# Two-layer S5 / RG-LRU / ConvFFN backbone: S5 parameters on stacked complex pairs, the last LRU tile beside the S5 gate, three modulation slots

## The chip, the cores and the metric

The kernel runs on one core of a Trainium2 chip. The metric is the device time of one execution in microseconds. "Before" and "after" name the two kernels. Engines: PE or TensorE (products), DVE or VectorE, ACT or ScalarE, POOL or GpSimd, SP or SyncE (which issues most of the DMAs).

## The reference

Two layers over 512 latent tokens with 256 context tokens ahead of them, width 1024. What matters here is the token mixing, which the reference computes so (cut):

```python
proj = h @ lw["w_in"]                       # u (512), x (512), g (512)
# S5: complex diagonal states, both directions
lam_bar = jnp.exp(lam * dt);  b_bar = ((lam_bar - 1.0) / lam)[..., None] * b_mat
s5_states = linear_scan(lam_bar, einsum(u, b_bar), s0, reverse)
# RG-LRU on x, both directions
xc = dwconv_seq(x_lru, conv_w, conv_b, LRU_PAD)
r, i = sigmoid(xc @ w_a + b_a), sigmoid(xc @ w_x + b_x)
log_a = (-LRU_C * r) * softplus(-lam);  a = jnp.exp(log_a)
lru_states = linear_scan(a, jnp.sqrt(-jnp.expm1(2.0 * log_a)) * (i * xc), h0, reverse)
y = gelu(s5_readout(s5_states, c_mat) + d * u)
y_s5 = y * sigmoid(y @ w_glu + b_glu)
y_lru = (lru_states[0] + lru_states[1]) * gelu(g_lru)
out = concatenate([y_s5, y_lru]) @ w_out
```

Then a post-norm, a gated feed-forward block with a 3x3 depthwise convolution, and another post-norm. Shifts, scales and gates of the norms come from `silu(c) @ w_mod + b_mod` (six vectors per layer and stream).

## The kernel before, in words

Products run as three fp32r products each (`mm3`, L165): a value is split into a high part, cast by ScalarE (L160), and a low part, the difference, by VectorE or GpSimd (L163). So L170, L171 and L172 are the three products of nearly all matrix work.

The kernel goes through its stages in order: features and modulation, token mixing of layer 0, output projection (`w_out`) and norm, the feed-forward block, and the same for layer 1. All on-chip buffers are slots of an arena (names such as `q0`, `t0`, `w6`, `e`); a slot's next user waits for its last.

S5 works in eight blocks of heads, `hb` 0 to 7. `enter` brings a block's inputs in, `prep(hb)` builds its small matrices (tables L595 to L600, a matrix that goes through DRAM as `td`), and `leave(hb)` (L714) does the complex scan: multiply by the rotations `cs` (L722 to L725, reloaded from DRAM `csd` through the one slot `t0`), two scans (L727), rotate back (L731, L732), write the states (L735 to L738), then 12 small products `yp` (L741 to L743), which ScalarE copies (L744). Every second block `store_y` sends the result to DRAM (`yd`, L648), from where the glu reloads it transposed (L962).

The RG-LRU works in four tiles l0 to l3 of 128 channels: gates by 16 products (L783) and sigmoids (L784), tanh and exp (L794, L795), root (L803), and on VectorE L798, L804, L807, scans (L809 to L812) and the sum of directions (L813); `gate` multiplies with the gelu of the projection g (L936). The projections are steps too: u0 to u3 for S5, x0 to x3 (with a convolution, L761), g0 to g3. `s` is `glu` (from L951): reload, gelu (L966), splits, then four times 24 products, two sigmoids (L977) and a multiplication (L978).

What is written where is set by the table `FILL`: one string per layer, with eight parts between bars; part hb is emitted behind `leave(hb)`. A scheduler then orders each engine's instructions by priorities: S5's blocks have 300 (`PRIO`), the fill steps none, so that the steps take the gaps of S5. Each engine, and each DMA queue, runs its list strictly in order. Between the steps a `filler` computes the modulation vectors: 16 loads of 512 KB of `w_mod` per pair of vectors through a ring of slots (m0, m1), each for four products (L185, L188).

`s5_params` (L442 to L578) makes the powers, tables and rotations of a layer: in layer 0 right at the start (`run(params, ...)`), in layer 1 chunk by chunk beside layer 0's feed-forward block. It works with real and imaginary parts as separate tiles of 128x32 and up, `cmul` (L261 to L266) being six operations; the rotations of each `hb` are six operations of 128x384 (L575 to L577).

Of the kernel before, what the change touches and what calls it, by code (L numbers as in the profile page):

```python
# [14 lines left out]
F32 = mybir.dt.float32  # L15
# [33 lines left out]
FILL = ('u1 x0 u2 u3|l0 x1||g0 l1 x2 g1|l2 x3|l3|g2|g3 s', 'x0 u1 u2 u3|l0 x1|g0 l1|x2 g1|l2 x3||l3|g3 g2 s')  # L49
# [3 lines left out]
def body(ctx: ExitStack, tc: tile.TileContext, a, out):  # L53
# [33 lines left out]
    def phase(side, *arenas):  # L87

        sides[side].close()
        pool = sides[side].enter_context(tc.tile_pool(name=side, bufs=1, side=side, reuse_waits="tile"))  # L90
        for dt, sizes in arenas:
            for n, kb in sizes.items():
                arena(pool, dt, **{n: kb})

    def mixing_phase():
        phase("left", (F32, several("a", 4, 4)), (F32, {"b": 8}))
        phase("right", (F32, several("q", 6, 3)), (F32, several("c", 2, 3)), (F32, {"w6": 4, "w7": 4}))
# [43 lines left out]
    def small(shape):  # L141
        count[0] += 1
        n = int(np.prod(shape[1:]))
        return cp.tile(list(shape), F32, name=f"{where[0]}_st_{count[0]}", tag=f"st{n}", bufs={12: 4, 4: 8, 1: 6}[n])
# [293 lines left out]
    prm = {"r8": const("r8", [128, 32]), "tab": const("tab", [128, 4, 32, 8]), "bb": const("bb", [128, 2, 33, 16]),  # L438
# [3 lines left out]
    def s5_params(l, scratch, raw_slots, phase_slots, cs_slots, tmp_slot, load=load):  # L442
# [14 lines left out]
        t = lambda: al(sh)  # L457
        (lre, lim, ldt), wre, wim = (lraw[:, i] for i in range(3)), t(), t()
        dt, are, th, mag, c1, s1, c8, s8 = (t() for _ in range(8))
        rr = dt  # L460
        t1, t2 = al([128, 32, 6]), al([128, 32, 6])
# [15 lines left out]
        reduce_angle(al, rr, th, sh)
        cos_sin(al, c8, s8, rr, sh)
# [28 lines left out]
        nr, den, q = t(), t(), t()  # L507
        V.tensor_scalar(nr, pw[:, 0, :, 1], -1.0, None, op0=ADD)
        ni = pw[:, 1, :, 1]
        V.tensor_mul(den, lre, lre)  # L510
        V.tensor_mul(q, lim, lim)
        V.tensor_add(den, den, q)
        V.reciprocal(den, den)
        V.tensor_mul(wre, nr, lre)
        V.tensor_mul(q, ni, lim)
        V.tensor_add(wre, wre, q)
        V.tensor_mul(wre, wre, den)
        V.tensor_mul(wim, ni, lre)
        V.tensor_mul(q, nr, lim)
        V.tensor_sub(wim, wim, q)  # L520
        V.tensor_mul(wim, wim, den)
        al.p = base
# [20 lines left out]
        V.tensor_copy(lo[:, 0, :, 1], c8)  # L543
        V.tensor_copy(lo[:, 1, :, 1], s8)
        v1, v2 = t1[:, :, 0], t2[:, :, 0]

        def square(o, x):
            cmul(o[0], o[1], x[0], x[1], x[0], x[1], v1, v2)
            return o

        x, y = (c8, s8), (wre, wim)
        square(y, x)
        grow(lo, 2, 0, 2, *y)
        square(x, y)
        grow(lo, 4, 0, 4, *x)
        square(y, x)
        V.tensor_copy(hi[:, 0, :, 1], y[0])
        V.tensor_copy(hi[:, 1, :, 1], y[1])
        square(x, y)
        grow(hi, 2, 0, 2, *x)  # L560
# [743 lines left out]
```

## Time and profile before

| | before |
|---|---|
| median of 3 runs | 1739.45 us (1738.14 to 1739.81) |
| profiled execution | 1738.61 us, span 1736.8 us |
| TensorE / VectorE / ScalarE / GpSimd busy | 1551.8 / 1287.7 / 672.1 / 522.7 us |
| mean granted TensorE clock | 0.938 of full |

The busy times are lengths of instructions within the span; matrix products overlap, so a busy TensorE is not one at its peak. The profiled execution is 0.84 us below the median. In the timeline a row is an instruction or a few equal ones on one engine: its start in us from the start of the span, its length, engine and line, then what it writes and reads. In square brackets stands how long the engine was idle ahead of it and what released it.

### The profile page before, as it was taken

How to read it: one execution, taken by the hardware profiler on the slowest of the kernel's cores; microseconds unless marked ns; L12 is line 12 of the kernel's file. 1: busy time of each engine (PE TensorE's matmuls, PEld its weight loads, DVE VectorE, ACT ScalarE, POOL GpSimd, SP SyncE). 2: the span in 40 equal slices, each digit the busy share in tenths (PEclk: the TensorE clock that was granted, in tenths of full speed). 3: DMA queues.
4: the chain of work that ended last, by engine and by line, in shares of the span. 5: the costliest groups of instructions: out<-in, count | busy, mean ns of one | idle time of the engine just before them, and what ended most of it. 6: DMA issues, size and time to landing. Idle time of an engine off the chain costs nothing. (4 is left out here: it accounts for less than half of the span.)

```text
span 1736.8 us, 22939 instructions
## 1 busy us (share of the span) xinstructions
PE 1551.8 (89%) x8824; PEld 1263.5 (73%) x8824; DVE 1287.7 (74%) x2244; ACT 672.1 (39%) x972; POOL 522.7 (30%) x328
## 2 busy tenths in 40 slices
PE   4997888498999999999999789989778999999996
PEld 1775666376988788887888668867456988888884
DVE  7998999368566997877689984888467575556587
ACT  3445566423633222222222236556651643323320
POOL 1000001318332222322326271000146444434374
PEclk8897888699899999999999998999879999999998
DMA  8365453522221212433334316765562233222231
GB/s 338 128 222 179 140 177 97 185 85 101 70 75 60 97 58 88 157 111 133 106 131 145 110 59 199 259 198 162 180 213 95 94 121 105 89 98 97 85 122 61
DMA packets 95358, 227.09 MB, mean 131 GB/s; under 512 B 28912, under 2 KB 39696, under 8 KB 95248
## 3 DMA queue, kind: packets, MB, share of 16 engines
q1 hardware_dynamic: 85456, 212.92, 36.6%
q10 hardware_dynamic: 9792, 12.71, 2.1%
q8 instruction: 69, 1.13, 0.3%
q14 instruction: 41, 0.34, 0.1%
HBM read 194.50 MB, written 31.10 MB: 130 GB/s over the span
## 5 line engine op out<-in xcount | busy, mean ns | idle before, releaser
L170 PE MATMUL banks<-ar,ar 128*128 128x512 f32 (+2 forms) x2152 | 774.9, 365 | 49.4 <-ACT ar L160 32.1
L171 PE MATMUL banks<-ar,ar 128*128 128x512 f32 (+2 forms) x2152 | 774.9, 361 | 16.8 <-DVE ar L396 13.1
L172 PE MATMUL banks<-ar,ar 128*128 128x512 f32 (+2 forms) x2152 | 767.8, 360 | 1.3 <-DVE ar L163 1.3
L163 POOL TENSOR_TENSOR ar<-ar,ar 128x1024 fp32r<-128x1024 f32 x148 | 364.9, 2473 | 672.8 <-ACT ar L160 596.1
L170 PEld LDWEIGHTS banks<-ar,ar 128*128 128x128 f32 x2152 | 411.1, 193 | 127.9 <-ACT ar L160 35.6
L171 PEld LDWEIGHTS banks<-ar,ar 128*128 128x128 f32 x2152 | 413.9, 192 | 80.8 <-DVE ar L396 15.1
L172 PEld LDWEIGHTS banks<-ar,ar 128*128 128x128 f32 x2152 | 413.8, 193 | 63.6 <-DVE ar L163 2.5
L160 ACT ACTIVATE ar<-ar 128x1024 fp32r<-128x1024 f32 (+2 forms) x248 | 238.9, 981 | 488.4 <-PE banks L171 212.3
L1143 DVE SCALAR_TENSOR_TENSOR ar<-banks,cols,ar 128x441 f32<-128x441 f32 (+2 forms) x352 | 243.6, 692 | 41.7 <-ACT ar L1138 35.1
L1177 DVE TENSOR_TENSOR ar<-banks,ar 128x512 f32<-128x512 f32 x160 | 109.4, 687 | 106.5 <-PE banks L172 104.5
L163 DVE TENSOR_TENSOR ar<-ar,ar 128x512 fp32r<-128x512 f32 (+2 forms) x100 | 113.6, 1148 | 81.0 <-ACT ar L160 64.3
L185 PE MATMUL banks<-ar,cond 128*32 128x256 f32 x192 | 65.9, 450 | 42.2 <-DMA ar<-in_w_mod_dram 42.2
L1150 ACT ACTIVATE ar<-ar,cols 128x768 f32<-128x768 f32 (+1 forms) x44 | 36.6, 831 | 130.5 <-DVE ar L1143 93.7
L826 POOL TENSOR_TENSOR ar<-ar 128x512 f32<-128x512 f32 x40 | 63.2, 1585 | 68.4 <-DVE ar L822 67.7
L185 PEld LDWEIGHTS banks<-ar,cond 128*32 128x32 f32 x192 | 16.2, 117 | 78.7 <-DMA ar<-in_w_mod_dram 59.6
L704 POOL MEMSET ar<- 128x8 f32 x16 | 1.9, 121 | 217.8 <-DVE ar L727 105.0
L188 PE MATMUL banks<-ar,cond 128*32 128x256 f32 x576 | 66.9, 450 | 0.0
L783 PE MATMUL banks<-ar,ar 128*128 128x512 f32 (+1 forms) x128 | 55.5, 563 | 10.3 <-ACT ar L925 5.7
L384 PE MATMUL banks<-ident,ar 128*128 128x128 f32 x176 | 36.0, 348 | 30.9 <-ACT ar L358 15.5
L396 DVE TENSOR_TENSOR ar<-ar,ar 128x256 fp32r<-128x256 f32 (+1 forms) x64 | 32.8, 531 | 31.8 <-ACT ar L395 31.7
L1138 ACT ACTIVATE ar<-banks,cols 128x512 f32<-128x512 f32 x44 | 29.9, 680 | 66.9 <-PE banks L172 66.8
L822 DVE TENSOR_TENSOR ar<-banks,ar 128x512 f32<-128x512 f32 x60 | 40.5, 681 | 18.7 <-PE banks L172 18.7
(243 smaller groups left out, 1723.3 us busy)
## 6 DMA issues: line engine op xcount, KB each, us to landing
ar<-in_w_mod_dram SPq DMA_DIRECT2D x96, 512.0 KB
ar<-in_ffn_w_up_dram SPq DMA_DIRECT2D x88, 512.0 KB
ar<-in_ffn_w_down_dram SPq DMA_DIRECT2D x44, 512.0 KB
ar<-in_w_in_dram SPq DMA_DIRECT2D x24, 512.0 KB
tabd<-ar SPq DMA_DIRECT2D x16, 512.0 KB
ar<-tabd SPq DMA_DIRECT2D x16, 512.0 KB
csd<-ar SPq DMA_DIRECT2D x16, 384.0 KB
ar<-csd SPq DMA_DIRECT2D x16, 384.0 KB
```

Source lines behind the costliest of these rows:

```text
L160: S.activation(hi, src, AF.Copy)
L163: return lo_eng.tensor_tensor(lo, src, hi.bitcast(F32), op=SUB)
L170: PE.matmul(ps, wh, xh, start=first and k == 0, stop=False)
L171: PE.matmul(ps, wh, xl, start=False, stop=False)
L172: PE.matmul(ps, wl, xh, start=False, stop=last and k == nk - 1)
L185: ins = PE.matmul(*args, **kw)
L188: ins = PE.matmul(*args, **kw)
L783: PE.matmul(gp, w[:, d, i, :], xc[:, o:o + n], start=True, stop=True)
L822: V.tensor_tensor(tmp, ps, g[:, cs], op=MUL)
L826: G.tensor_tensor(xs_t[:, cs], xs_t[:, cs], tmp, op=ADD)
L1143: inst[0] = V.scalar_tensor_tensor(av[:, yo, xo], uv[:, yi, xi], tap(1 + dy, 1 + dx, ch), av[:, yo, xo], op0=MUL, op1=ADD)
L1177: V.tensor_tensor(acc, ps, acc, op=ADD)
```

## The change

1. `s5_params` works on pairs: real and imaginary parts stand in one tile, and exp, angle, cosine and sine run on the pair of powers 1 and 8 at once. A complex product (`times`) is two multiplications over both parts and two sums; a square is three operations. Copies into the table are four for eight. For layer 0 (`sets=2`) a rotation step makes two blocks: 24 operations of 768 columns where 48 of 384 stood; `cs` lies in slot `e`, in two halves, and goes out in two stores.
2. `FILL`: in layer 0, l3 (part 5) and g2 (part 6) move into part 7, where g3 and the glu are. In layer 1, l3 moves from part 6 to 7 and g2 from 7 to 5.
3. In part 7 the products of the projections are tied behind the last product of `leave(7)`; `lru` is a generator: l3's gates are emitted at once, the rest (`lru_rest`) inside `glu`, behind the last gelu.
4. The modulation ring gets a third slot, `w7`; the gates of the LRU lose it (seven for eight).
5. `columns` takes its scratch from slot `f0`; q3, q4 and q5 become one tile; one small buffer fewer; `prep(0)` of layer 0 has a priority.

```diff
-FILL = ('u1 x0 u2 u3|l0 x1||g0 l1 x2 g1|l2 x3|l3|g2|g3 s', 'x0 u1 u2 u3|l0 x1|g0 l1|x2 g1|l2 x3||l3|g3 g2 s')
+FILL = ('u1 x0 u2 u3|l0 x1||g0 l1 x2 g1|l2 x3|||l3 g2 g3 s', 'x0 u1 u2 u3|l0 x1|g0 l1|x2 g1|l2 x3|g2||l3 g3 s')
...
+        def times(o, x, mre, mim, u1, u2):
+            V.tensor_tensor(u1, x, mre, op=MUL)
+            V.tensor_tensor(u2, x[:, ::-1], mim, op=MUL)
+            V.tensor_tensor(o[:, 0], u1[:, 0], u2[:, 0], op=SUB)
+            V.tensor_tensor(o[:, 1], u1[:, 1], u2[:, 1], op=ADD)
...
-            cmul(o[0], o[1], x[0], x[1], x[0], x[1], v1, v2)
+            v = t1[:, :, :, 0]
+            V.tensor_tensor(v, x, x, op=MUL)
+            V.scalar_tensor_tensor(o[:, 1], x[:, 0], 2.0, x[:, 1], op0=MUL, op1=MUL)
+            V.tensor_sub(o[:, 0], v[:, 0], v[:, 1])
...
-            cs = new(cs_slots[hb % 2], [128, 2, 4, 96])
-            tt = new(tmp_slot, [128, 2, 4, 96])
+            if sets > 1:
+                cs = new(cs_slots, [128, 2, 2, ng, 96])[:, h // sets % 2]
+            else:
+                cs = new(cs_slots[h % 2], [128, 2, ng, 96])
+            tt = new(tmp_slot, [128, 2, ng, 96])
...
-            nc.sync.dma_start(csd[l, hb], cs.rearrange("p i g n -> p (i g n)"))
+            for j in range(sets):
+                nc.sync.dma_start(csd[l, h + j].rearrange("p (i x) -> p i x", i=2),
+                                  cs[:, :, 4 * j:4 * j + 4].rearrange("p i g n -> p i (g n)"))
...
-            self.gates = ring(*(f"q{i}" for i in range(6)), "w6", "w7")
+            self.gates = ring(*(f"q{i}" for i in range(6)), "w6")
...
-    params = s5_params(0, "t", ("a2", "t0"), ("w6", "w7"), ("q3", "q4"), "q5", S.dma_start)
+    params = s5_params(0, "t", ("a2", "t0"), ("w6", "w7"), "e", "q3", 2, S.dma_start)
...
-        md_r = ring("m0", "m1")
+        md_r = ring("m0", "m1", "w7")
-        filler = itertools.chain(*(mods(l, q, md_r, md_r, md_b, after=first_w) for q in (1, 2)))
+        filler = itertools.chain(*(mods(l, q, md_r, md_r, md_b, 3, after=first_w) for q in (1, 2)))
+        tie = [None]
...
+            with behind(tie[0]):
+                return products(lat, ctxt, w, tag, do_ctx, parts)
...
             with tc.high_priority(PRIO2[l]):
-                hs[m] = lru(m, xcs[m], gate_b)
+                it = lru(m, xcs[m], gate_b)
+                next(it)
+            if tie[0] is None:
+                lru_rest(it, m)
+            else:
+                rest.append((it, m))
...
-                S.activation(yt, yt, AF.Gelu_apprx_tanh, bias=zero)
+                gelu = S.activation(yt, yt, AF.Gelu_apprx_tanh, bias=zero)
+            for it, m in rest:
+                with behind(gelu):
+                    lru_rest(it, m)
...
-                s5.leave(hb, fo2, tm)
+                left = s5.leave(hb, fo2, tm)
...
+                tie[0] = left if hb == 7 else None
```

Three places show how this moves the instructions. The lines of the changed kernel are its own: L726 to L742 are L722 to L738 of before, L804 to L819 are L798 to L813, L1004 and L1005 are L977 and L978.

First, VectorE at the start of layer 0's `leave(7)`, before:

```order
L809 SCALAR_TENSOR_TENSOR ar_88<-ar_82,ar_83 128x256
L812 SCALAR_TENSOR_TENSOR ar_89<-ar_84,ar_85 128x768
L810 SCALAR_TENSOR_TENSOR ar_88<-ar_82,ar_88,ar_83 128x512
L722 TENSOR_TENSOR ar_68<-ar_68 128x768
L723 TENSOR_TENSOR ar_68<-ar_68 128x768
L813 TENSOR_TENSOR ar_88<-ar_88,ar_89 128x768
L163 TENSOR_TENSOR ar_67<-ar_68,ar_67 128x1024
L724 TENSOR_TENSOR ar_68<-ar_68 128x384
L725 TENSOR_TENSOR ar_68<-ar_68 128x384
L936 TENSOR_TENSOR ar_68<-ar_68,ar_80 128x768
L727 SCALAR_TENSOR_TENSOR ar_68<-ar_68 128x384 x2
L731 TENSOR_TENSOR ar_68<-ar_68 128x768
```

and in the changed kernel:

```order
L741 TENSOR_TENSOR ar_68<-ar_68 64x4x32
L742 TENSOR_TENSOR ar_68<-ar_68 64x4x64
L726 TENSOR_TENSOR ar_68<-ar_68 128x768
L727 TENSOR_TENSOR ar_68<-ar_68 128x768
L688 TENSOR_TENSOR ar_68<-banks,dd_112 128x16
L728 TENSOR_TENSOR ar_68<-ar_68 128x384
L729 TENSOR_TENSOR ar_68<-ar_68 128x384
L731 SCALAR_TENSOR_TENSOR ar_68<-ar_68 128x384 x2
L735 TENSOR_TENSOR ar_68<-ar_68 128x768
L736 TENSOR_TENSOR ar_68<-ar_68 128x768
```

Ahead of `leave(7)` (768-wide L722, now L726) the scans of l3 no longer stand, and inside it neither L813, L163 nor the gate's product L936; `prep`'s L688 has moved into it.

Second, the glu of layer 0. VectorE in the changed kernel, between the first and second multiplications by the sigmoid (L1005):

```order
L1005 TENSOR_TENSOR ar_68<-ar_68 128x768
L810 SCALAR_TENSOR_TENSOR ar_81<-ar_83,ar_81 128x768
L810 SCALAR_TENSOR_TENSOR ar_82<-ar_86,ar_82 128x768
L813 TENSOR_TENSOR ar_83<-ar_83,ar_81 128x768
L813 TENSOR_TENSOR ar_80<-ar_80,ar_82 128x768
L815 SCALAR_TENSOR_TENSOR ar_81<-ar_83 128x256
L818 SCALAR_TENSOR_TENSOR ar_82<-ar_86,ar_80 128x768
L816 SCALAR_TENSOR_TENSOR ar_81<-ar_83,ar_81 128x512
L819 TENSOR_TENSOR ar_81<-ar_81,ar_82 128x768
L1005 TENSOR_TENSOR ar_68<-ar_68 128x768
L948 TENSOR_TENSOR ar_68<-ar_68,ar_81 128x768
```

and ScalarE at the same place (L801 is l3's exp, L809 its root, L1004 the glu's sigmoid, L163 casts):

```order
L801 ACT_TABLE_LOAD
L801 ACTIVATE ar_83<-ar_83,lru_st_2274,coef_41_524 128x768
L801 ACTIVATE ar_86<-ar_86,lru_st_2274,coef_41_524 128x768
L1004 ACT_TABLE_LOAD
L1004 ACTIVATE ar_68<-banks,cols_40_491 128x384 x2
L807 ACTIVATE lru_st_2282<-ar_86 128x1
L809 ACT_TABLE_LOAD
L809 ACTIVATE ar_81<-ar_81,lru_st_2282 128x768
L809 ACTIVATE ar_82<-ar_82,lru_st_2282 128x768
L163 ACTIVATE ar_66<-ar_68 128x1024
L163 ACTIVATE ar_67<-ar_68 128x1024
```

l3's rest now stands between the glu's multiplications; on ScalarE the glu's first two sigmoids stand between l3's exp and its root, each with a table load (ACT_TABLE_LOAD).

Third, SyncE's queue in the tail of layer 0 (`yd` is the S5 output, `gd` the modulation vectors), before:

```order
L834 DMA ar_68<-gd_107 128x1024
L200 DMA ar_68<-in_w_out_s_dram 128x1024
L962 DMA ar_68<-yd 128x8x96
L834 DMA ar_68<-gd_107 128x1024
L1037 DMA ar_68<-in_x_dram 128x1024
L200 DMA ar_68<-in_w_out_lru_dram 128x1024 x2
L962 DMA ar_68<-yd 128x8x96
L200 DMA ar_68<-in_w_out_lru_dram 128x1024 x2
```

and in the changed kernel:

```order
L694 DMA ar_76<-td 128x1x128 x4
L840 DMA ar_68<-gd_105 128x1024
L985 DMA ar_68<-yd 128x8x96
L840 DMA ar_68<-gd_105 128x1024
L985 DMA ar_68<-yd 128x8x96
L203 DMA ar_68<-in_w_out_s_dram 128x1024
L1066 DMA ar_68<-in_x_dram 128x1024 x2
L203 DMA ar_68<-in_w_out_s_dram 128x1024 x2
```

The last reload of the S5 output stood behind two loads of `in_w_out_lru` and stands ahead of them now.

## Rows read from the trace of the kernel before

**Rows 1.** The page: its span, and busy time by engine.
```profile
span 1736.8 us, 22939 instructions
...
PE 1551.8 (89%) x8824; PEld 1263.5 (73%) x8824; DVE 1287.7 (74%) x2244; ACT 672.1 (39%) x972; POOL 522.7 (30%) x328
```

**Rows 2.** Windows: length, busy us (count) of PE, weights, DVE, ACT, POOL; clock; DMA; GB/s.
```profile
286.50:295.50 9.00, 8.90 (x53) 7.70 (x52) 9.00 (x11) 6.30 (x9) 0.00 (x0) 1.00 0.18 45
300.00:350.00 50.00, 21.41 (x98) 19.50 (x99) 20.93 (x18) 18.51 (x25) 19.63 (x8) 0.64 0.49 161
340.00:358.00 18.00, 17.69 (x96) 16.37 (x95) 7.49 (x9) 9.76 (x15) 0.02 (x1) 1.00 0.16 56
550.00:600.00 50.00, 45.91 (x244) 38.60 (x243) 47.00 (x137) 14.97 (x19) 12.13 (x5) 1.00 0.20 65
...
1250.00:1300.00 50.00, 32.01 (x210) 23.23 (x203) 28.20 (x29) 32.66 (x44) 22.74 (x9) 0.76 0.62 214
```

**Rows 3.** Timeline, VectorE: start, us, engine, line, work [idle before <- what ended it].
```profile
262.83 0.95 DVE L722 TENSOR_TENSOR ar<-ar 128x768 f32<-128x768 f32 x1
...
284.36 1.83 DVE L804 SCALAR_TENSOR_TENSOR ar<-ar,ar 128x768 f32<-128x768 f32 x2 [3.81 <-ACT ar L803]
...
291.35 0.94 DVE L722 TENSOR_TENSOR ar<-ar 128x768 f32<-128x768 f32 x1
...
299.59 3.10 DVE L732 TENSOR_TENSOR ar<-ar 128x768 f32<-128x768 f32 x1
302.61 3.96 DVE L163 TENSOR_TENSOR ar<-ar,ar 128x768 fp32r<-128x768 f32 x2
...
308.48 0.42 DVE L738 TENSOR_TENSOR ar<-ar 64x256 f32<-64x256 f32 x1
```

**Rows 4.** Timeline, TensorE, the two long gaps of layer 0's tail.
```profile
307.82 0.72 PE L742 MATMUL banks<-ar,ar 128*128 128x96 f32 x2 [11.88 <-DVE ar L738]
...
331.58 1.01 PE L170 MATMUL banks<-ar,ar 128*128 128x384 f32 x2 [18.06 <-ACT ar L160]
```

**Rows 5.** Timeline, ScalarE, layer 0's tail.
```profile
282.10 1.28 ACT L803 ACT_TABLE_LOAD   x1
283.40 1.76 ACT L803 ACTIVATE ar<-ar,lru_st 128x768 f32<-128x768 f32 x2
...
313.56 0.49 ACT L744 ACTIVATE ar<-banks 128x384 f32<-128x384 f32 x1 [0.98 <-PE banks L743]
...
327.39 3.41 ACT L966 ACTIVATE ar<-ar,glu_st 128x768 f32<-128x768 f32 x4
...
340.26 1.05 ACT L977 ACTIVATE ar<-banks,cols 128x384 f32<-128x384 f32 x2 [3.33 <-PE banks L172]
```

**Rows 6.** Timeline, SyncE's queue, layer 0's tail.
```profile
322.69 0.39 SPq L962 DMA_DIRECT2D ar<-yd  x1
```

**Rows 7.** Timeline, GpSimd, beside layer 0's last `leave`.
```profile
298.93 5.95 POOL L163 TENSOR_TENSOR ar<-ar,ar 128x1024 fp32r<-128x1024 f32 x2 [24.51 <-ACT ar L160]
```

**Rows 8.** Timeline, VectorE, the end of layer 0's glu.
```profile
360.70 2.67 DVE L163 TENSOR_TENSOR ar<-ar,ar 128x512 fp32r<-128x512 f32 x2 [1.22 <-ACT ar L160]
```

**Rows 9.** Timeline, VectorE, layer 1: two `leave`s at their closest.
```profile
1089.17 0.96 DVE L722 TENSOR_TENSOR ar<-ar 128x768 f32<-128x768 f32 x1
...
1096.90 1.23 DVE L163 TENSOR_TENSOR ar<-ar,ar 128x1024 fp32r<-128x1024 f32 x1
...
1100.26 0.96 DVE L722 TENSOR_TENSOR ar<-ar 128x768 f32<-128x768 f32 x1
```

**Rows 10.** Timeline, TensorE, waits for modulation weights in layer 1's tail.
```profile
1226.49 0.63 PE L185 MATMUL banks<-ar,cond 128*32 128x256 f32 x1 [3.60 <-DMA ar<-in_w_mod_dram]
...
1254.36 0.63 PE L185 MATMUL banks<-ar,cond 128*32 128x256 f32 x1 [3.57 <-DMA ar<-in_w_mod_dram]
...
1258.65 0.64 PE L185 MATMUL banks<-ar,cond 128*32 128x256 f32 x1 [3.21 <-DMA ar<-in_w_mod_dram]
```

**Rows 11.** Groups by line and form, VectorE, 20 to 110 us, rotations.
```profile
L576 DVE TENSOR_TENSOR ar<-ar,ar 128x384 f32<-128x384 f32 x7 | 3.6, 552 | 0.0
```

More of the change, by code (lines that the diff above doesn't have):

```diff
@@ L90, in phase @@
         pool = sides[side].enter_context(tc.tile_pool(name=side, bufs=1, side=side, reuse_waits="tile"))
-        for dt, sizes in arenas:
+        for dt, sizes, *one in arenas:
+            if one:
+                arena(pool, dt, **sizes)
+                continue
             for n, kb in sizes.items():
@@ L143, in small @@
         n = int(np.prod(shape[1:]))
[L144 removed]
+        return cp.tile(list(shape), F32, name=f"{where[0]}_st_{count[0]}", tag=f"st{n}", bufs={12: 3, 4: 8, 1: 6}[n])
     load = nc.sync.dma_start
@@ L456, in s5_params @@
         al = Stack(new(scratch, [128, 2048]))
[L457 to L461, printed above, removed]
+        pair = [128, 2, 32]
+        dt, den = al(sh), al(sh)
+        pa = al([128, 2, 2, 32])
+        ang, pole, w, ws = (al(pair) for _ in range(4))
+        c18 = al([128, 2, 2, 32])
+        t1, t2 = (new(tmp_slot, [128, 2, 2, 32, 6])[:, i] for i in range(2))
         base = al.p
@@ L517, in s5_params @@
[L517 to L522, printed above, removed]
+        ri = pw[:, :, :, 1]
+        V.tensor_scalar(ri[:, 0], ri[:, 0], -1.0, None, op0=ADD)
+        V.tensor_tensor(w, lraw[:, 0:2], lraw[:, 0:2], op=MUL)
+        V.tensor_add(den, w[:, 0], w[:, 1])
+        V.reciprocal(den, den)
+        lam = [lraw[:, i].unsqueeze(1).to_broadcast(pair) for i in range(2)]
@@ L552, in s5_params @@
+        x, y = w, ws
+        square(y, p8)
+        grow(lo, 2, 0, 2, y)
+        square(x, y)
+        grow(lo, 4, 0, 4, x)
+        square(hi[:, :, :, 1], x)
+        square(x, hi[:, :, :, 1])
+        grow(hi, 2, 0, 2, x)
         square(y, x)
-        grow(lo, 2, 0, 2, *y)
+        grow(hi, 4, 0, 4, y)
         square(x, y)
[L555 to L560, printed above, removed]
@@ L894, in proj, with products @@
             ctxt = ctx_b() if do_ctx else None
+            with behind(tie[0]):
+                return products(lat, ctxt, w, tag, do_ctx, parts)
+        def products(lat, ctxt, w, tag, do_ctx, parts):
             if do_ctx and l > 0:
@@ L942, in x_part, with lru_rest @@
             xcs[m] = lru.conv4(m, lat, ctxt)
+        rest = []
         def lru_part(m):
             with tc.high_priority(PRIO2[l]):
-                hs[m] = lru(m, xcs[m], gate_b)
+                it = lru(m, xcs[m], gate_b)
[4 more added lines that the diff above has]
+                rest.append((it, m))
+        def lru_rest(it, m):
+            where[0] = f"lru{l}"
+            hs[m] = next(it)
             gate(m)
@@ L990, in body @@
         with behind(tail[0] if l == 0 else None):
-            ready = {0: s5.prep(0)}
+            with tc.high_priority(2 * PRIO[l]) if l == 0 else nullcontext():
+                ready = {0: s5.prep(0)}
             if l == 0:
```

110 lines of the change are left out of this document (48 added, 62 removed).

## The prediction

> **What bounds the kernel now.** I read the page first, for who is busy: TensorE works 1551.8 of 1736.8 us [rows 1]. What can be won is therefore in the few stretches where it stands still. The table of windows finds them: between 300 and 350 us TensorE is busy for 21.41 us and VectorE for 20.93, at a granted clock of 0.64; between 1250 and 1300 us TensorE for 32.01 at 0.76 [rows 2]. Both are the same place in the two layers: the end of the S5 chain, the glu behind it, and the output projection that can't begin before the glu is done. Last I read the timelines of that place, engine by engine.
>
> In layer 0 VectorE begins `leave(6)` at 262.83 but `leave(7)` only at 291.35, and writes its last state at 308.48 + 0.42 = 308.9 [rows 3]. In between it does the rest of the last LRU tile (l3). Before that it even waits 3.81 us for ScalarE's square root, and inside `leave(7)` two splits of a gate product take 3.96 us. TensorE has run out of other work and waits 11.88 us for the last state [rows 4]. The S5 output is copied at 313.56 to 314.05 [rows 5]; its last reload is issued only at 322.69 [rows 6], since SyncE's queue holds two loads of w_out ahead of it that wait for a free slot. Gelu follows at 327.39 [rows 5], and TensorE, idle for 18.06 us, starts the glu at 331.58 [rows 4]. The first sigmoid runs at 340.26 [rows 5]; from there the glu's 96 products fill TensorE, 17.69 of 18 us at full clock [rows 2]. The last split ends at 360.70 + 2.67 = 363.4 [rows 8]. From the last state to the end of the glu: 363.4 - 308.9 = 54.5 us.
>
> **The change, part by part, against the profiled execution (1738.61 us, span 1736.8; the median of the runs is 0.84 higher).**
>
> *The last LRU tile behind the S5 chain, layer 0.* From the start of `leave(6)` on, VectorE no longer does l3's rest, the gates' products or the splits of g2 and g3. The new order keeps two `leave`s and four small operations of `prep`. A `leave` costs 1096.90 - 1089.17 = 7.7 us at its least [rows 9]; layer 0 adds the context's two operations (8.2), and the four are 2.3 together: 18.7 us. Where VectorE has nothing else, two `leave`s have started 1100.26 - 1089.17 = 11.1 us apart [rows 9], because the second needs its reloaded rotations; 262.83 + 11.1 + 7.7 = 281.6, the same place. Before, the stretch took 308.9 - 262.8 = 46.1. The most to win is thus 27 us, the least 11: the 7.0 us from 284.36 to 291.35 and the two splits' 3.96 [rows 3], if other waits eat the rest. With both orders priced instruction by instruction by their forms' durations, VectorE's work ahead of `leave(6)` is equal within 1 us (what the parameters save, l2's rest, now earlier, takes), so its start stays. The waits that stood there were l3's, so I stay near the upper end and put the last state at 283.5: **-25 us**.
>
> *What comes back in the glu.* TensorE now does g2 and g3, 96 products, between the last S5 product and the glu; 53 such products took 8.90 us at full clock [rows 2], so some 16. Its 18.06 us of idle time cover them. The reload of the S5 output stands ahead of the w_out loads: it was issued 322.69 - 314.05 = 8.6 us behind the copy, and I take 6 of these off. So 12 to 13 us behind the last state gelu can run, if g2's product is done, which it is at 4.7 (yp and copy, 313.56 - 308.9) + 8 = 13. Then I follow ScalarE's new order, from last state to end: four gelus 3.41 [rows 5], four casts 3.6, tanh 1.8, the gate's gelu and five casts 6, a table load and exp 3.1, a table load 1.28: the first sigmoid at about 33, where it was 340.26 - 308.9 = 31.4. Then it puts a table load, l3's square root (1.28 + 1.76 [rows 5]), two weight casts and one more table load, 6.4 us in all, between the first tile's two sigmoids and the next: at 41. From then on TensorE's four last groups of 12 products and the sigmoids, 96 products in 17.7 us [rows 2] or 2.2 us a group, need 9: 50. l3's rest on VectorE (7.0 us [rows 3] and four 768-wide operations at 0.95) runs from 35 to 46 and a cast of its gated tile stands in ScalarE's queue ahead of the last sigmoids: some 3 us more. With the last multiplication and splits, 5 us, the end is at 58 to 60, against 54.5. I take **+5 us**, bounds -4 (the reload's 6 won, two table loads lost) and +20 (l3's 9 us on ScalarE and 10.8 on VectorE all in a row). Layer 0: -25 + 5 = -20.
>
> *The parameters.* For layer 0 the rotations shrink from 48 operations of 384 columns to 24 of 768: by length 48 x 0.552 [rows 11] against 24 x 0.95 [rows 3], 3.7 us. Squares and small products on stacked pairs give some 3 more. As said, this is in the -25: the first `leave`s don't move. The stores of rotations become two per step, 16 requests as before, but in three-level form; they stand ahead of nothing that ends last. In layer 1 the parameters run beside the first feed-forward block, where TensorE loses 50 - 45.91 = 4.1 us in the window with VectorE's 137 instructions [rows 2]. Fewer instructions can give back 0 to 4: **-1 us**. The scratch of `columns`, the arena of three slots as one tile, one small buffer fewer and seven gate slots for eight only move waits on buffers; VectorE's queue of mixing work covers these.
>
> *Layer 1.* TensorE waits 3.60, 3.57 and 3.21 us for modulation weights in this tail, 10.4 together [rows 10]. A third slot lets a load start one step earlier. g2 starts earlier and l3's rest goes behind gelu, but here `leave(7)` has no l3 rest ahead of it to lose, and g3 stands in TensorE's order between the first products of the glu. Bounds: -10.4 (all these waits gone) and +16 (layer 0's +20, less the root and its table loads of some 4 us, which stood ahead of gelu and go behind it). I take **-3 us**: between the two, nearer to the waits, which I can see.
>
> Sum: -20 - 1 - 3 = -24 us; 1738.61 - 24 = 1714.6, and 0.8 more for the median: **1715 us**.
>
> **One rule against it.** L732 on VectorE took 3.10 us where an equal operation takes 0.95, and the two splits behind it 3.96, while GpSimd ran two splits for 5.95 us from 298.93 on [rows 3, 7]: 2.15 us lost for one meeting. The Trainium skill (SBUF — State Buffer, "Who interferes with whom") says that a VectorE instruction with two SBUF inputs and a GpSimd instruction that reads SBUF lock each other out, so that the second waits for the whole of the first. By that rule, the trace agrees. For this change it bears on l3's rest, all of two inputs, which now runs while GpSimd splits w_out; with the four meetings of rival A the sum would be 1728.
>
> **Rivals.**
> *A, the glu eats more.* GpSimd's splits of w_out's four LRU rows, 2.97 us each [rows 7], all meet l3's rest, in both layers, and delay the last sigmoids through the cast of its tile: 4 x 2.15 = 8.6 us, of which the forecast has about 2: +6.5 per layer, 1728. For it: in ScalarE's new order the casts that release these splits stand among the same sigmoids. Against it: VectorE is idle in much of the glu.
> *B, slower.* The glu becomes a chain through ScalarE: TensorE waits for one of two banks, the bank for a sigmoid, the sigmoid in ScalarE's queue behind the cast that waits for l3's rest. Then the moved pieces add up: 9 + 10.8 + 8.6 = 28.4 us against 25 won in layer 0, +3; in layer 1, which wins only the 4 us ahead of gelu, +24: 1739 + 3 + 24 = 1766. It decides once more than 25 us of the moved work stands on the path. For it: only two banks serve the glu. Against it: tanh, exp and root need nothing from the glu, and only one cast waits for l3's rest.
> *C, more.* The last state comes at 282 and the glu gives back 2 instead of 5, and layer 1 loses all 10.4 us of its waits: 1738.6 - 25 - 1 - 10.4 + 0.8 = 1703.
> *D, nothing moves.* `leave(7)` waits for something else until nearly 300 us: its reloaded rotations, its features, or TensorE, which has l3's gates ahead of the last two steps; or l3's gates hold VectorE up before `leave(6)`. Within 3 us of 1739.
>
> **How the numbers follow.** The forecast has 0.50, A 0.18, B 0.09, C 0.17, D 0.06. About 0.2% is what a measurement of this kernel can tell from no change. The forecast, A and C are faster: 0.85; D is the same: 0.06; B is slower: 0.09. The range runs from just under C, 1699, to where D begins, 1736; it leaves out B, D and the low part of C.
>
> **What would show it.** Right: the last state of layer 0 at 281 to 286 us; TensorE's 11.88 us under 5, its 18.06 filled by g2's and g3's products; gelu within 14 us of the last state (18.5 before); the last split of the glu at 340 to 347; l3's rest between the first and second multiplication; in layer 1 smaller waits for modulation weights. Wrong: `leave(7)` still over 20 us behind `leave(6)`, a glu that ends over 65 us behind the last state, or sigmoids that wait on VectorE for over 5 us. From the output projection on, the parts should take the same time in both kernels, but for the parameters' window.

## The result, and the profile after

The changed kernel takes 1699.89 us (median of 4 runs, 1698.41 to 1702.49), the kernel before on the same chips 1738.80 (4 runs, 1735.66 to 1739.81): a ratio of 0.9781, 95% interval 0.9763 to 0.9799, or 39 us less. The forecast was 1715, with a range of 1699 to 1736: the measured time lies 0.9 us above its lower end. The profiled execution took 1698.41 us, 40.2 less than the one before. The page of the changed kernel (answers to [rows 1]), then three windows (to [rows 2]):

```profile
span 1696.6 us, 22763 instructions
...
PE 1541.2 (91%) x8824; PEld 1259.8 (74%) x8824; DVE 1266.2 (75%) x2072; ACT 672.2 (40%) x970; POOL 525.1 (31%) x328
```

```profile
300.00:350.00 50.00, 32.72 (x133) 28.36 (x132) 35.49 (x31) 31.77 (x41) 24.08 (x8) 0.77 0.43 146
550.00:600.00 50.00, 46.17 (x235) 39.05 (x234) 38.73 (x85) 12.27 (x14) 12.41 (x5) 0.97 0.26 84
1250.00:1300.00 50.00, 45.49 (x202) 35.56 (x200) 39.74 (x58) 14.94 (x17) 34.67 (x19) 1.00 0.46 159
```

Between 300 and 350 us TensorE now works 32.72 us where it worked 21.41, and the clock is 0.77 for 0.64; between 1250 and 1300 it works 45.49 for 32.01 (that window now holds the output projection). The window of layer 1's parameters has 85 VectorE instructions for 137, and TensorE works only 0.26 us more in it.

To say where the time went I read six moments of each trace from the timelines: the last state of each layer's S5 chain, the first multiplication of the output projection's result by its gate (VectorE L822 before, L828 after: the first residual), the first residual behind layer 0's feed-forward block, and the last one of all. All are of profiled executions. From here on, the tail of a layer is the time from its last state to its first residual.

| us | before | after | difference |
|---|---|---|---|
| last state, layer 0 | 308.9 | 278.0 | -30.9 |
| from there to the first residual | 55.1 | 70.1 | +15.0 |
| from there to the end of layer 0's feed-forward | 635.7 | 636.4 | +0.7 |
| from there to the last state of layer 1 | 214.1 | 209.8 | -4.3 |
| from there to the first residual | 87.0 | 66.2 | -20.8 |
| from there to the last residual | 425.2 | 425.4 | +0.2 |

Both tails moved, in opposite ways. Layer 0 won 30.9 us ahead of the last state and gave 15.0 back; layer 1 won 20.8 in its tail, where I had foreseen almost nothing.

Layer 0's tail on VectorE in the changed kernel (answers to [rows 3, 8]; L726 to L742 are the `leave`, L1005 the glu's multiplication, L813 and L815 of l3's rest, L948 its gate, L166 splits):

```profile
255.68 0.95 DVE L726 TENSOR_TENSOR ar<-ar 128x768 f32<-128x768 f32 x1
...
269.06 0.96 DVE L726 TENSOR_TENSOR ar<-ar 128x768 f32<-128x768 f32 x1 [2.71 <-ACT ar L619]
...
277.56 0.42 DVE L742 TENSOR_TENSOR ar<-ar 64x256 f32<-64x256 f32 x1
...
311.90 0.96 DVE L1005 TENSOR_TENSOR ar<-ar 128x768 f32<-128x768 f32 x1 [6.55 <-ACT ar L1004]
...
315.98 4.01 DVE L813 TENSOR_TENSOR ar<-ar,ar 128x768 f32<-128x768 f32 x2
319.91 2.88 DVE L815 TENSOR_TENSOR_SCAN ar<-ar 128x256 f32<-128x256 f32 x1
...
327.40 0.95 DVE L948 TENSOR_TENSOR ar<-ar,ar 128x768 f32<-128x768 f32 x1
...
334.20 6.39 DVE L166 TENSOR_TENSOR ar<-ar,ar 128x512 fp32r<-128x512 f32 x6 [0.77 <-ACT ar L163]
...
342.71 4.70 DVE L166 TENSOR_TENSOR ar<-ar,ar 128x512 fp32r<-128x512 f32 x2 [1.26 <-ACT ar L163]
348.03 1.29 DVE L828 TENSOR_TENSOR ar<-banks,ar 128x512 f32<-128x512 f32 x2 [0.62 <-PE banks L175]
```

`leave(7)` starts at 269.06 where it started at 291.35, and waits only 2.71 us, for a copy on ScalarE (L619). The last state comes at 277.56 + 0.42 = 278.0, and the last split of the glu ends at 342.71 + 4.70 = 347.4, 69.4 us behind it. Then look at the lengths: two L813 take 4.01 us (0.95 each alone, as e8 shows below), the 256-wide scan L815 2.88, the six splits at 334.20 6.39 (5.23 before) and the last two 4.70 (2.67 before, [rows 8]). ScalarE at the same time (answers to [rows 5]; L989 gelu, L1004 the glu's sigmoids, L163 casts), and GpSimd (to [rows 7]):

```profile
293.11 3.42 ACT L989 ACTIVATE ar<-ar,glu_st 128x768 f32<-128x768 f32 x4
...
310.81 1.05 ACT L1004 ACTIVATE ar<-banks,cols 128x384 f32<-128x384 f32 x2
...
318.24 1.05 ACT L1004 ACTIVATE ar<-banks,cols 128x384 f32<-128x384 f32 x2
...
328.39 2.74 ACT L163 ACTIVATE ar<-ar 128x768 fp32r<-128x768 f32 x3 [6.55 <-DVE ar L948]
331.03 1.03 ACT L1004 ACTIVATE ar<-banks,cols 128x384 f32<-128x384 f32 x2
```

```profile
316.06 6.20 POOL L166 TENSOR_TENSOR ar<-ar,ar 128x1024 fp32r<-128x1024 f32 x2 [6.20 <-ACT ar L163]
330.25 5.44 POOL L166 TENSOR_TENSOR ar<-ar,ar 128x1024 fp32r<-128x1024 f32 x2 [8.00 <-DVE ar L166]
338.87 4.86 POOL L166 TENSOR_TENSOR ar<-ar,ar 128x1024 fp32r<-128x1024 f32 x1 [3.17 <-ACT ar L163]
344.11 2.83 POOL L166 TENSOR_TENSOR ar<-ar,ar 128x1024 fp32r<-128x1024 f32 x1 [0.37 <-ACT ar L163]
```

The first sigmoid stands 310.81 - 278.0 = 32.8 us behind the last state and the second tile's 40.2, as followed in the prediction (33 and 41). Then a cast waits 6.55 us for L948, and the sigmoid behind it runs only at 331.03. GpSimd splits w_out from 316.06 to 322.26, beside the long L813 and L815, from 330.25, and from 338.87 to 346.94, beside the last splits. On TensorE the two long gaps of this tail before (11.88 and 18.06 us, [rows 4]) are gone, but two waits for sigmoids stand in the glu (L173 is one of the three products):

```profile
311.45 0.69 PE L173 MATMUL banks<-ar,ar 128*128 128x384 f32 x1 [7.72 <-ACT ar L1004]
...
331.64 0.69 PE L173 MATMUL banks<-ar,ar 128*128 128x384 f32 x1 [6.26 <-ACT ar L1004]
```

In layer 1 before, SyncE's last reload of the S5 output (L962), then ScalarE (L784 the sigmoids of l3's gates, L794 and L803 l3's tanh and root, L966 gelu):

```profile
1224.67 0.38 SPq L962 DMA_DIRECT2D ar<-yd  x1
```

```profile
1242.75 0.69 ACT L784 ACTIVATE ar<-banks,cols 128x512 f32<-128x512 f32 x1 [4.26 <-PE banks L783]
...
1243.71 1.95 ACT L794 ACTIVATE ar<-ar,lru_st,coef 128x768 f32<-128x768 f32 x2
...
1258.11 1.76 ACT L803 ACTIVATE ar<-ar,lru_st 128x768 f32<-128x768 f32 x2
...
1261.19 2.56 ACT L966 ACTIVATE ar<-ar,glu_st 128x512 f32<-128x512 f32 x4
```

and after (L652 the store of the S5 output, L800 and L809 l3's tanh and root, L989 gelu):

```profile
1197.19 0.56 ACTq L652 DMA_DIRECT2D yd<-ar  x1
...
1208.24 1.33 ACT L989 ACTIVATE ar<-ar,glu_st 128x512 f32<-128x512 f32 x2
...
1212.67 1.33 ACT L989 ACTIVATE ar<-ar,glu_st 128x512 f32<-128x512 f32 x2
...
1224.29 1.94 ACT L800 ACTIVATE ar<-ar,lru_st,coef 128x768 f32<-128x768 f32 x2
...
1237.36 1.76 ACT L809 ACTIVATE ar<-ar,lru_st 128x768 f32<-128x768 f32 x2
```

Before, gelu ran at 1261.19, 47.4 us behind the last state (1213.8), with the sigmoids of l3's gates (which wait for TensorE's products until 1242.75), l3's tanh, exp and root in front of it. The reload that it needs had been issued at 1224.67. Now it runs at 1208.24, 14.0 us behind the last state (1194.2), and tanh and root follow it.

### The profile page after: what moved, and what is told of

It reads as the page before. It is cut to its first block, busy times and chain, and to the rows that moved or that the text cites. A ratio compares the mean times of both kernels' runs of the same rounds, so it can differ in the third digit from the quotient of the medians.

```text
span 1696.6 us, 22763 instructions
## 1 busy us (share of the span) xinstructions
PE 1541.2 (91%) x8824; PEld 1259.8 (74%) x8824; DVE 1266.2 (75%) x2072; ACT 672.2 (40%) x970; POOL 525.1 (31%) x328
## 4 chain that ended last, share of the span: by engine, by line
PE 53%; DVE 26%; DMA 7%; ACT 6%; issue 3%; POOL 3%; SPq 0%; ACTq 0%; POOLq 0%; DVEq 0%
PE banks L173 16%; PE banks L175 15%; PE banks L174 15%; DVE ar L1172 3%; DMA ar<-in_w_mod_dram 2%; DVE ar L166 2%; ACT ar L163 2%; POOL ar L832 1%; PE banks L188 1%; PE banks L788 1%; DVE ar L1211 1%; DVE ar L836 1%; DVE ar L578 1%; DVE ar L1206 1%; PE banks L706 1%
## 5 line engine op out<-in xcount | busy, mean ns | idle before, releaser
L173 PE MATMUL banks<-ar,ar 128*128 128x512 f32 (+2 forms) x2152 | 775.5, 366 | 49.9 <-ACT ar L1004 16.1
L166 POOL TENSOR_TENSOR ar<-ar,ar 128x1024 fp32r<-128x1024 f32 x148 | 368.2, 2495 | 648.0 <-ACT ar L163 633.3
L173 PEld LDWEIGHTS banks<-ar,ar 128*128 128x128 f32 x2152 | 410.7, 192 | 129.5 <-ACT ar L1004 18.4
L163 ACT ACTIVATE ar<-ar 128x1024 fp32r<-128x1024 f32 (+3 forms) x248 | 239.2, 980 | 488.7 <-PE banks L174 219.5
L166 DVE TENSOR_TENSOR ar<-ar,ar 128x512 fp32r<-128x512 f32 (+2 forms) x100 | 108.9, 1104 | 83.1 <-ACT ar L163 65.5
L188 PE MATMUL banks<-ar,cond 128*32 128x256 f32 x192 | 61.4, 428 | 16.8 <-DMA ar<-in_w_mod_dram 16.8
L191 PE MATMUL banks<-ar,cond 128*32 128x256 f32 x576 | 62.8, 428 | 0.0
L788 PE MATMUL banks<-ar,ar 128*128 128x256 f32 (+1 forms) x128 | 50.6, 515 | 8.6 <-ACT ar L789 3.6
L188 PEld LDWEIGHTS banks<-ar,cond 128*32 128x32 f32 x192 | 16.1, 114 | 53.1 <-DMA ar<-in_w_mod_dram 31.9
L1167 ACT ACTIVATE ar<-banks,cols 128x512 f32<-128x512 f32 x44 | 29.9, 680 | 62.5 <-PE banks L175 62.4
L828 DVE TENSOR_TENSOR ar<-banks,ar 128x512 f32<-128x512 f32 x60 | 40.5, 681 | 18.0 <-PE banks L175 18.0
```

Of the source, the lines that this page charges most:

```text
L163: S.activation(hi, src, AF.Copy)
L166: return lo_eng.tensor_tensor(lo, src, hi.bitcast(F32), op=SUB)
L173: PE.matmul(ps, wh, xh, start=first and k == 0, stop=False)
L188: ins = PE.matmul(*args, **kw)
L191: ins = PE.matmul(*args, **kw)
L788: PE.matmul(gp, w[:, d, i, :], xc[:, o:o + n], start=True, stop=True)
```

## The experiments

Each was timed beside the kernel before on the same chip. The times "to the first residual" are of profiled executions. My theory was that the order in the two tails is the gain; its parts were taken one by one.

**The two halves of the change.** e1 is the kernel before with edits 1 and 5; e2 the kernel before with edits 2 to 4:

```diff
 e1:  FILL, LRU, md_r and tie as before;  s5_params, columns, arena, prep(0) as changed
 e2:  s5_params, columns, arena, prep(0) as before;  FILL, LRU, md_r and tie as changed
```

> The kernel before with the new S5 parameters alone (stacked pairs, rotations by two sets, the columns' scratch, the arena of three slots, prep(0)'s priority); fill table, LRU and modulation slots as before. Theory 1 (the order of the two tails is the gain, the parameters only save VectorE some 5 us that other work takes up): 1728 to 1736 us, 3 to 11 under before; first leave some 5 us earlier, last state of layer 0 at 300 to 307 (308.9 before), layer 1's tail as before. Theory 2 (VectorE freed at the start moves everything behind it and is a large part of the gain): under 1724.

> The kernel before with the new order alone (fill table, l3's rest behind gelu, the tie, three modulation slots), parameters as before. Theory 1: 1702 to 1710 us, most of the 39 us; last state of layer 0 at 280 to 286. Theory 2: over 1715. If the two parts add up, before less this and before less the parameters alone make together the 39 us within 4.

e1: 1733.06 us, ratio 0.9974 (0.9958 to 0.9990). e2: 1704.11, ratio 0.9824 (0.9800 to 0.9848); the kernel before beside them 1736.13. So 3.1 and 32.0 us, together 35.1 of the 39 foreseen to add up within 4. Theory 2 falls: the parameters are a small gain. In e1 the first `leave` starts at 102.0 for 108.9, but the last state comes only 3.4 us earlier: between 268 and 304 us six of VectorE's instructions meet GpSimd (a meeting is an instruction of VectorE that runs beside a split of weights there) and take 12.5 us more than their forms do alone; before, two such meetings took 4.2. e10, below, shows their rows.

**The third modulation slot.**

```diff
-        md_r = ring("m0", "m1", "w7")
+        md_r = ring("m0", "m1")
-        ... mods(l, q, md_r, md_r, md_b, 3, after=first_w)
+        ... mods(l, q, md_r, md_r, md_b, 2, after=first_w)
```

> The changed kernel with two modulation slots again. Theory 1a (the third slot ends TensorE's waits for modulation weights in layer 1's tail, 10.4 us before): 1707 to 1712, with waits of 3 us each back in that stretch. Theory 1b (the waits went because the modulation steps stand at other places in TensorE's order): within 2 us of 1700.

e3: 1703.85 us, ratio 0.9823 (0.9798 to 0.9847), between the two. The waits decide. The groups of the modulation products on TensorE from 1100 to 1300 us, before, and in e3 (there L188; the last columns are the idle time ahead and what ended it):

```profile
L185 PE MATMUL banks<-ar,cond 128*32 128x256 f32 x56 | 19.9, 454 | 17.4 <-DMA ar<-in_w_mod_dram 17.4
```

```profile
L188 PE MATMUL banks<-ar,cond 128*32 128x256 f32 x52 | 16.0, 399 | 2.6 <-DVE modc L331 1.7 <-DMA ar<-in_w_mod_dram 0.9
```

With two slots again the waits for these loads stay at 0.9 us where they were 17.4 (3.4 in the changed kernel), and layer 1's tail is 64.1 us, not longer than 66.2. It is not the slot that ended these waits. In e1, with the old order, they are 17.2 us, so the new order ended them; by which of its edits is not shown. Theory 1a falls. Whether the slot is worth the remaining 0.4% is open: the two ratios' intervals just overlap.

**Layer 1's order.**

```diff
-'... |x2 g1|l2 x3|g2||l3 g3 s'
+'... |x2 g1|l2 x3||l3|g3 g2 s'
```

> The changed kernel with the fill table's old string for layer 1: l3 at once in part 6, g3 and g2 ahead of the glu. Theory 1c (layer 1's 20 us come from gelu no longer standing behind l3's chain on ScalarE): 1712 to 1722, gelu again 40 us or more behind layer 1's last state (14 in the changed kernel). Theory 1a (they come from the third slot): 1700 to 1706.

e4: 1707.81 us, ratio 0.9849 (0.9819 to 0.9879). In ScalarE's timeline gelu is late again:

```profile
1241.82 1.28 ACT L989 ACT_TABLE_LOAD   x1
1243.11 2.56 ACT L989 ACTIVATE ar<-ar,glu_st 128x512 f32<-128x512 f32 x4
```

1243.11 is 46.0 us behind the last state (1197.1), and the tail takes 80.6 us for 66.2. So this string is worth 14.4 us of the tail's 20.8 in the profiled execution, 8 by the medians and 12 by the ratios: the time falls short of the 1712 to 1722 expected of theory 1c. Of theory 1c the mechanism holds: with l3 in part 6 all its work is emitted at once and stands on ScalarE ahead of gelu. The other 6.4 us of the tail stay won with the old string (the tie of the projections is still in); that was not tried by itself. With this string, as in e5 below, l3's work takes the slot of l2's sum before the gate has read it, here in layer 1; the instructions are the same in kind and number.

**Layer 0's order.** e5 restores layer 0's string. In it, with seven gate slots, l3's work takes the slot of l2's sum before the gate has read it, so that l2's rows of y_lru come out of other data; the instructions are the same in kind and number. e9 has the same spread without that: g2 ahead of l3. e10 is e9 without the tie in layer 0.

```diff
 e5
-'... |l2 x3|||l3 g2 g3 s'
+'... |l2 x3|l3|g2|g3 s'
 e9
+'... |l2 x3|g2|l3|g3 s'
 e10: as e9, and
-                tie[0] = left if hb == 7 else None
+                tie[0] = left if hb == 7 and l > 0 else None
```

> The changed kernel with the fill table's old string for layer 0: l3, rest and all, in part 5, g2 in 6, g3 in 7. Theory 3 (putting l3 and the gates behind the S5 chain wins some 27 us on the last state, but gives 15 back in the glu): 1708 to 1714 us; last state of layer 0 at 300 to 307, glu to output projection 51 to 56 us. Rival (layer 0's gain is the early start and the freed VectorE, not the order): 1698 to 1704.

> The changed kernel with the work of layer 0 spread again (g2 in part 5, l3 with its rest in part 6, g3 in part 7, still tied); layer 1 and the rest as changed. Theory 6 (layer 0's new place for l3 wins some 12 us on the last state and loses 16 in the tail, so on balance it costs; the gain up to the output projection comes from the parameters, the tie of g3 and the slots): 1691 to 1697 us, first residual of layer 0 at 341 to 346 (348.0 changed, 364.0 before). Theory 3 (the new place is what wins): over 1703.

> The kernel of the run just before, without the tie in layer 0: g3's products may run ahead of the last S5 products again. Theory 7 (the tie keeps g3 and the splits behind it out of the last leave, which is worth about 9 us): 1699 to 1706 us, last state of layer 0 at 296 to 304. Rival (the tie orders what would run so anyway): within 2 us of the run before.

e5: 1693.74 us, ratio 0.9743 (0.9707 to 0.9778). This is under both expectations, and theory 3 falls: with l3 back in the S5 chain the kernel is not slower. Its last state comes at 289.9, its first residual at 343.7, earlier than the changed kernel's 348.0. Hence theory 6 and e9: 1691.00 us, ratio 0.9724 (0.9695 to 0.9754), last state 286.6, first residual 339.9. So the new place of l3 and g2 wins 8.6 us on the last state and loses 16.8 in the tail (70.1 for 53.3). On balance it costs layer 0 8 us.

e10: 1710.38 us, ratio 0.9836 (0.9805 to 0.9866). The tie is worth 19 us, twice what I expected, and the time is above both expectations. VectorE in e10 in the last two `leave`s (L603 is `prep`), GpSimd beside it, and VectorE in e9's last `leave`:

```profile
281.55 2.76 DVE L603 TENSOR_TENSOR ar<-tab,cc 128x512 f32<-128x512 f32 x1
...
293.58 2.70 DVE L728 TENSOR_TENSOR ar<-ar 128x384 f32<-128x384 f32 x1
...
302.51 2.58 DVE L739 TENSOR_TENSOR ar<-ar 64x384 f32<-64x384 f32 x1
305.10 2.34 DVE L741 TENSOR_TENSOR ar<-ar 64x128 f32<-64x128 f32 x1
...
308.59 0.42 DVE L742 TENSOR_TENSOR ar<-ar 64x256 f32<-64x256 f32 x1
```

```profile
267.49 6.13 POOL L166 TENSOR_TENSOR ar<-ar,ar 128x1024 fp32r<-128x1024 f32 x2 [6.91 <-ACT ar L163]
...
292.88 5.61 POOL L166 TENSOR_TENSOR ar<-ar,ar 128x1024 fp32r<-128x1024 f32 x2 [9.12 <-ACT ar L163]
302.20 5.09 POOL L166 TENSOR_TENSOR ar<-ar,ar 128x1024 fp32r<-128x1024 f32 x2 [3.72 <-ACT ar L163]
```

```profile
279.51 0.56 DVE L728 TENSOR_TENSOR ar<-ar 128x384 f32<-128x384 f32 x1
...
285.38 0.55 DVE L739 TENSOR_TENSOR ar<-ar 64x384 f32<-64x384 f32 x1
...
286.15 0.42 DVE L742 TENSOR_TENSOR ar<-ar 64x256 f32<-64x256 f32 x1
```

Without the tie g3 and all behind it run early, and GpSimd splits eight weight tiles between 267 and 307 us, inside the S5 chain. Each time VectorE loses about 2.1 us: L728 takes 2.70 where e9's takes 0.56, L739 2.58 for 0.55, eight such meetings in all, some 17 us. The last state comes at 309.0, as late as before (308.9), 22.4 us behind e9's. Most of what the tie does there, 17 of the 22.4 us, is to keep GpSimd out of that chain.

**The loss in layer 0's glu.** e6 puts the cast that waits for L948 behind the last sigmoid, e7 all of l3's rest, e8 takes the w_out weights' splits from GpSimd:

```diff
 e6, e7:  sig[0] = S.activation(sg..., ps, AF.Sigmoid, ...)
 e6
+            with behind(sig[0] if m == 3 else None):
                 split(ge[0][:, m, 0:ntok], ylru[m][0]..., ylru[m][1]..., V)
 e7: from behind the gelus to behind the glu's splits
+            for it, m in rest:
+                with behind(sig[0]):
+                    lru_rest(it, m)
 e8
-        lo_eng[0] = G
+        lo_eng[0] = V
...
+        lo_eng[0] = G        # behind the loads of w_out
```

> The changed kernel with one thing moved: the cast and split of l3's gated tile stand behind the glu's last sigmoid, in both layers. Theory 4 (the glu's 15 us of loss are ScalarE's queue: this cast waits for l3's rest on VectorE with three sigmoids behind it): 1688 to 1694 us, first residual of layer 0 60 to 64 us behind the last state (70.1 in the changed kernel), of layer 1 60 to 63 (66.2). Theory 5 (the loss is VectorE's own work and its meetings with GpSimd; the sigmoids only wait beside it): 1697 to 1701.

> The changed kernel with all of l3's rest (tanh, exp, root, VectorE's operations, the cast) behind the glu's last sigmoid; the output projection needs it only in its second pass, over the LRU rows. Theory 4: 1672 to 1684 us; first residual of layer 0 48 to 53 us behind the last state, of layer 1 52 to 58. Theory 5 foresees the same here, unless the second pass then waits for l3's tile or for the weights cast behind it: 1690 to 1700 in that case.

> The changed kernel with the low parts of all w_out weights on VectorE and none on GpSimd in the glu. If VectorE and GpSimd lock each other out, l3's products, its first scan and the last splits fall back to their lengths alone (L813 0.95 each where two took 4.01, the 256-wide scan 0.69 for 2.88), against 8 weight splits of 1.22 more per layer on VectorE: Theory 5 1692 to 1698 us, Theory 4 1698 to 1706.

e6: 1697.86 us, ratio 0.9759 (0.9737 to 0.9782), the same as the changed kernel within the intervals; the first residual is 70.0 us behind the last state, as without the edit. Theory 4 falls: the cast in the queue of sigmoids is not what ends the tail.

e8: 1684.81 us, ratio 0.9686 (0.9663 to 0.9708), 15 us better and under the 1692 to 1698 of theory 5. On VectorE:

```profile
313.37 0.95 DVE L813 TENSOR_TENSOR ar<-ar,ar 128x768 f32<-128x768 f32 x1
...
315.37 0.95 DVE L813 TENSOR_TENSOR ar<-ar,ar 128x768 f32<-128x768 f32 x1
...
317.38 0.69 DVE L815 TENSOR_TENSOR_SCAN ar<-ar 128x256 f32<-128x256 f32 x1
...
338.23 1.29 DVE L828 TENSOR_TENSOR ar<-banks,ar 128x512 f32<-128x512 f32 x2 [0.59 <-PE banks L175]
```

L813 and L815 have fallen to 0.95, 0.95 and 0.69, as foreseen, though VectorE has more to do. The first residual is 62.4 us behind the last state, layer 1's 62.5 for 66.2. Theory 5 holds: the meetings of VectorE and GpSimd are what this tail loses most to, up to the last splits of the glu, which stood beside GpSimd's last weights (338.87 to 346.94). Without them 7.6 of the 15.0 us come back, though VectorE has the weights' splits to do; the other half is not explained by this run.

e7: 1698.41 us, ratio 0.9764 (0.9739 to 0.9789), as theory 5 has it where the second pass waits. In layer 0 it did nearly what it should: 54.8 us to the first residual for 48 to 53, and the feed-forward block ends 11.2 us earlier than in the changed kernel. In layer 1, whose tail is 66.1 us as in the changed kernel, it was lost again. ScalarE (casts of l3's tile, then of an LRU weight), and TensorE in the two passes of layer 1's output projection:

```profile
1262.51 2.54 ACT L163 ACTIVATE ar<-ar 128x512 fp32r<-128x512 f32 x3 [12.36 <-DVE ar L948]
1270.92 1.06 ACT L163 ACTIVATE ar<-ar 128x1024 fp32r<-128x1024 f32 x1 [5.87 <-DMA ar<-in_w_out_lru_dram]
```

```profile
1252.71 0.65 PE L173 MATMUL banks<-ar,ar 128*128 128x512 f32 x1 [4.78 <-DVE ar L828]
...
1274.47 0.51 PE L174 MATMUL banks<-ar,ar 128*128 128x512 f32 x1 [1.36 <-POOL ar L166]
...
1277.40 0.51 PE L174 MATMUL banks<-ar,ar 128*128 128x512 f32 x1 [0.55 <-POOL ar L166]
```

The cast of l3's tile waits 12.36 us for its gate, the casts of the LRU rows' weights stand behind it, and the second pass waits for their splits on GpSimd, 1.9 us in all; in the first pass TensorE waits 4.78 us for the first residual, which stands among l3's operations on VectorE. From the first to the last residual it then took 437.7 us for 425.4; the rest of these 12 us was not traced (this profiled execution was 1702.18 us, 4 above its median, so not all of that is the edit's).

**The two put together.** e11 is e9 with e8's edit; e12 the changed kernel with e8's edit and e7's in layer 0 alone.

> Layer 0's work spread as in e9, and the w_out weights split on VectorE alone in both layers. If the two gains are separate (e9's in front of the last state's tail, the weights' in the glu and the output projection's second pass): 1677 to 1684 us. If they are the same one (both only keep l3's rest from meeting GpSimd): 1684 to 1690.

> The changed kernel with the w_out weights split on VectorE, and in layer 0 alone l3's rest behind the glu's last sigmoid. In e7 this ended layer 0's feed-forward block 11 us earlier, in the weights' run 10.5 us earlier. Separate: 1675 to 1680 us; the same gain twice: 1682 to 1687, since the output projection's second pass then waits for l3's tile.

e11: 1683.87 us, ratio 0.9689 (0.9654 to 0.9725), where the two expectations meet (1684): the weights' edit is worth 7 us on top of e9 for 15 without it. That there is less to meet with l3 out of the glu fits this, but was not traced. e12: 1677.77, ratio 0.9651 (0.9620 to 0.9683), separate gains as foreseen (1675 to 1680) and the fastest of all: 22 us under the changed kernel, 61 to 64 under the one before. Its last state comes at 275.7, its first residual at 329.7 (54.1 later).

## Why the prediction was right, and where it was off

The direction held and the range just held; the gain was 39 us for 24. The sum came as near as it did partly by luck: layer 0's first term came near its size for another reason than the one given, its second was 10 us too small, and layer 1's term, the largest miss, had the wait that mattered at nothing. By its steps:

- **The last LRU tile behind the S5 chain: -25, measured -30.9.** From the start of `leave(6)` to the last state it takes 22.3 us (255.7 to 278.0) where 20.7 was said and 46.1 stood before. The start of `leave(6)` "stays", I wrote; it came 7.1 us earlier. But the reason is not the one that I gave. I had put all of it on the work that VectorE no longer does there. With l3 back in the chain and g2 ahead of it e9 still ends at 286.6, so that their new place is 8.6 of the 30.9. The tie is worth 22.4 on the last state in e10, most of it meetings with GpSimd's splits, of which the kernel before had only two in this stretch (L732 and the two splits behind it, [rows 3, 7], 4.2 us); the parameters alone are 3.4 (e1). These three do not add up: without the tie more splits stand in the chain than before, six meetings in e1 and eight in e10.
- **What comes back in the glu: +5, measured +15.0 to the first residual.** The glu ends 69.4 us behind the last state where 58 to 60 was said; over 65 was one of my signs of being wrong, and a cast that waits 6.55 us for VectorE ahead of a sigmoid is another (over 5). The steps on ScalarE held to within 1 us up to the second tile's sigmoid. The term that was mis-sized is the meetings with GpSimd: I had about 2 us of them. The two L813 lost 2.1, L815 2.2, and the last two splits took 2.0 more than before (4.70 for 2.67, [rows 8]); that is some 4 us over what I had, and what the other 6 of the 10 us are is not separated. It is rival A's mechanism, with meetings of 6.3 us in these rows for its 8.6, but not with the weights that it named: two of w_out's S5 rows met l3's rest, and the LRU rows, loaded later, the glu's last operations. The Trainium skill's rule (SBUF — State Buffer, "Who interferes with whom"), that of a VectorE instruction with two SBUF inputs and a GpSimd instruction that reads SBUF the second waits for the whole of the first, fits what e8 and e10 show. The trace agrees: the eight instructions of 0.29 to 1.3 us that were caught in e10 each lost 2.0 to 2.2, whatever their own length, where a GpSimd split that meets nothing takes 2.34 to 2.40.
- **Layer 0 in sum: -20, measured -15.9** to the first residual.
- **The parameters: inside the -25, and -1 in the feed-forward block.** e1: 3 us in all. From layer 0's first residual to the end of its feed-forward block, where I had -1, the changed kernel took 0.7 us more.
- **Layer 1: -3, measured -25.** This is the step that failed. "Here `leave(7)` has no l3 rest ahead of it to lose" was right, and I priced only the waits for modulation weights. But the profile of before had gelu 47.4 us behind the last state in layer 1 and 18.5 in layer 0; ScalarE ran the sigmoids of l3's gates, tanh, exp and root in between, in its order, and gelu needed none of them. The reload that it does need was issued at 1224.67; in layer 0 of the changed kernel such a reload was there 3.3 us after its issue (issued 289.55, its first reader on ScalarE at 292.87), so I estimate that gelu could have run at about 1228. I had traced that order for layer 0 alone. The lower bound of -10.4 was therefore no bound. e4 loses 14.4 us of the tail's 20.8 by restoring the string. The other 6.4, and the 4.3 us ahead of layer 1's last state, were not traced to one edit.
- **The third slot.** Named as what would end the waits; e3 shows that it is not.
- Rival B's time did not come, but a part of its mechanism did: TensorE waits 7.72 and 6.26 us for sigmoids, the second behind the cast that waits for l3's rest. e6, which moves that cast, gains nothing by it, so that it is not what ends the tail. Rival C had layer 1's waits for weights gone, and most of them went: in this tail they are 14.4 us before and 3.4 after. But in e4 9 of these 14.4 are gone too, and its tail is still 80.6, so that these 9 can be at most 6.4 of the 20.8. D fell with `leave(7)` at 269.1.

## What to carry to other kernels

When work is moved off a chain, look on ScalarE, VectorE and each queue for what stands in order ahead of the chain's next step without being needed by it, in every layer: here gelu stood behind another tile's gates and root in one layer and not in the other, and the order that let it go first was worth 8 to 14 us. And before spreading element-wise work over VectorE and GpSimd side by side, look for rows of one form with two lengths: each meeting cost VectorE some 2 us, and moving eight splits per layer onto VectorE itself, which then had more to do, was 15 us faster.

## What the runs showed that I had not expected

The cost of a meeting does not grow with VectorE's instruction: a 64x128 operation of 0.29 us took 2.34 and a 768-wide one 3.10, both beside GpSimd splits of about 2.5 to 3.2. So a chain of many short VectorE instructions loses the larger share of its time by it: e10's S5 chain lost 17 us to eight splits, which took 23 us there of an engine that was otherwise idle. And a tie in the order of TensorE's products was worth 19 us, mostly because it moved when another engine's splits come free.
